# Earlier loads of the raw output weights, and two queued operations a step, in an encoder block

## The chip, the cores and the metric

The kernel runs on one core of a Trainium2 chip. The metric is the device time of one execution in microseconds. The median of three executions before the change is 499.15 us (498.17, 499.15, 500.5).

## What is computed

One encoder layer on 1024 tokens of width 1024, in float32. A combined projection is cut into head groups: group A is 2-D neighbourhood attention with 8 heads on a 16 x 64 grid, group B is windowed attention with 8 query and 2 key heads. Each group's output is gated, then projected, added to the input and normalised:

```python
h = jnp.einsum('bsd,de->bse', x, w_in[layer])
q_a, k_a, v_a, z_a, q_b, k_b, v_b, z_b = jnp.split(h, SPLIT_POINTS, axis=-1)
y_a = neighborhood_attention(q_a, k_a, v_a, rel_pos_bias[layer])
y_b = windowed_gqa_with_sink(rotary(q_b), rotary(k_b), v_b, sink_logits[layer])
mixed = jnp.concatenate([y_a * silu(z_a), y_b * silu(z_b)], axis=-1)
y = jnp.einsum('bse,ed->bsd', mixed, w_out[layer])
x = layer_norm(DEEPNORM_ALPHA * x + y, ln_gain[layer], ln_bias[layer])
```

(The reshapes into heads are left out here.)

## The kernel before

Every large float32 product is made of three matmuls in a reduced float format: each operand is split into a high part (a cast) and a low part (operand minus high part), and high x high, high x low and low x high are summed. So a weight has to be loaded raw, cast by ScalarE and subtracted by GpSimd or VectorE before TensorE (PE) can use it.

After a first stage (the value projection), the kernel walks 128 attention units of 128 queries each, first those of group B, then those of group A, with a software pipeline over steps i = 0 to 134. In step i:
- PE makes the scores of unit i (lines 532 and 533), the product of probabilities and values of unit i-6 (line 596), and after it a share of the "fill", matmuls that have nothing to do with the attention (`pump_to`).
- VectorE (DVE) adds the bias and finds the row maximum of unit i (line 539), and makes the low half of the probabilities of unit i-1 (line 566, "split-low").
- ScalarE (ACT) makes the high half of the probabilities of unit i-1 (line 565), scales the output of unit i-6 (line 601) and takes the exponential of unit i (line 554).
- SyncE (SP) issues every DMA in the listed order: biases four steps ahead, value windows (`va`), and for each unit a DMA transpose of the split probabilities (line 569), which line 596 needs five steps later.

The schedule is written out by hand (`tc.manual_schedule()`): every engine executes its instructions in the order in which the program emits them.

Beside this fixed frame there are four queues of small operations, for ScalarE, VectorE, GpSimd (POOL) and SyncE. `enq` puts an operation in its queue with the operations that it depends on; `pop(eng, n)` emits at most n of those that are ready, by priority, and an operation is ready when all that it depends on was emitted in an earlier step. ScalarE's queue is popped at the end of a step, behind the exponential; VectorE's behind the split-low; SyncE's queue gives one load at the start of a step, unless a bias or a value window was issued there, and then only if the load has waited over two steps. `need` emits an operation at once, where a matmul is about to use its result.

The fill is in this order: the last of the 21 column projections, `z3`, takes the steps 112 to 119 (6 matmuls a step). Then come three "heads" of the output projection, `out_head`: the first three of the eight row groups of `w_out`, in the order 4, 5, 6 (`EO`), for token tiles 0, half of 3, and 1. The first head takes the steps 120 to 125 with 3 matmuls a step, so each of these steps uses one new half of a row group: n = 0 in step 120, up to n = 5 in step 125. For each n:
- `wo_load(n)` loads the raw half (256 KB, tile `wor`, line 652), queued at step `WO_LD[n]`. The raw tiles take the places of `w_in`'s tiles (`WO_TAG`).
- `wo_split(n)`, queued at step 116 + n for n = 0 to 5, makes the high part `woh` on ScalarE (line 661) and the low part `wol` on GpSimd, or on VectorE where n is 2 or 5 (line 665).
- `m_queue(e)`, queued at the steps `M_AT`, splits the gated outputs of the row group e on ScalarE (line 680, two casts) and GpSimd (line 681).

n = 6, 7 and 8 are loaded in the loop too, but are split behind it. Behind the loop, `final` splits the other parts and makes the remaining output projection, the residual and the normalisation. Its matmuls begin with the heads for token tile 2 in the banks `ps_t`.

The two halves of `z3` are evacuated through ScalarE's queue (line 262) and VectorE (line 263) before PE may reuse their bank `ps_pj`; the second half of the first head (n = 1 is its first matmul) waits for the second of them.

## Time and profile before

| | value |
|---|---|
| median of three runs | 499.15 us |
| profiled execution | 498.68 us, span 496.9 us |
| PE matmul busy | 479.3 us (96%) |
| VectorE busy | 319.2 us (64%) |
| ScalarE busy | 279.6 us (56%) |
| GpSimd busy | 163.2 us (33%) |
| DMA | 74.74 MB, mean 150 GB/s |
| chain that ended last | PE 92% of the span |

The page cuts the span into 40 slices of 12.4 us. Each digit is the busy share in tenths; `PEclk` is the clock that was granted to PE, in tenths of full speed.

```profile
PE   8999999999999999999999999999998599999993
PEclk9999999999999999999999999999999579999997
DMA  8860001595285554847798989999799549204612
```

PE has one hole, in the slices 31 and 32 of the 40, that is 373 to 397 us, and the clock is low in the second of them and in the slice behind it. The end of the attention loop lies in this stretch: the steps 117 to 134 run from 371 to 411 us.

The waits between 360 and 497 us name the same lines (who waits and for what: us in total, times, longest):

```profile
PE ps_pj L698 <- ACT woh L661: 5.6, 3, 2.6
PEld ps_pj L698 <- POOL wol L665: 2.1, 2, 1.1
PE ps_pj L698 <- POOL wol L665: 1.1, 2, 0.6
PE ps_pj L698 <- DVE z L263: 0.8, 1, 0.8
```

"PE ... <- ACT woh L661" reads: a matmul of line 698 stood idle until ScalarE's cast of line 661 had ended.

### The profile page before, as it was taken

The numbers are of one execution on the slowest core, as the hardware profiler recorded it, in microseconds if no ns is written. First come the engines' busy times: TensorE is split into PE (matmuls) and PEld (weight loads), VectorE is DVE, ScalarE is ACT, GpSimd is POOL, SyncE is SP. The second block draws the span as 40 slices with busy tenths as digits, with TensorE's granted clock in tenths as the row PEclk, the third lists the DMA queues.
The fourth block names the chain that finished last, engine by engine and source line by source line (L and its number), as shares of the span: only waits on it lengthen the run. The fifth ranks groups of instructions, "written<-read, shape, count | busy, mean of one in ns | idle before, by whom it ended". The sixth has DMA issues, their size and how long they took to land.

```text
span 496.9 us, 9312 instructions
## 1 busy us (share of the span) xinstructions
PE 479.3 (96%) x3240; PEld 396.1 (80%) x3240; DVE 319.2 (64%) x788; ACT 279.6 (56%) x723; POOL 163.2 (33%) x152
## 2 busy tenths in 40 slices
PE   8999999999999999999999999999998599999993
PEld 7999988887887778878788788888886378888883
DVE  5718216778578778787777667656666239659545
ACT  5641133423788778888787878767788434012102
POOL 0030012695254174552133143123253204306423
PEclk9999999999999999999999999999999579999997
DMA  8860001595285554847798989999799549204612
GB/s 259 286 234 0 1 21 44 158 289 162 65 132 118 128 108 102 143 108 137 176 184 176 191 182 230 204 210 232 146 213 233 110 116 306 102 1 149 219 56 85
DMA packets 132383, 74.74 MB, mean 150 GB/s; under 512 B 101104, under 2 KB 117488, under 8 KB 132080
## 3 DMA queue, kind: packets, MB, share of 16 engines
q1 hardware_dynamic: 132192, 74.00, 62.7%
q8 instruction: 25, 0.41, 0.3%
q14 instruction: 22, 0.18, 0.1%
q10 hardware_dynamic: 144, 0.15, 0.1%
HBM read 43.72 MB, written 9.96 MB: 108 GB/s over the span
## 4 chain that ended last, share of the span: by engine, by line
PE 92%; DVE 3%; ACT 1%; issue 1%; POOL 1%; DMA 1%; SPq 0%; POOLq 0%; DVEq 0%; ACTq 0%
PE ps_pj L291 45%; PE ps_s L698 7%; PE ps_t L596 7%; PE ps_pj L698 5%; PE ps_t L698 4%; PE ps_s L361 4%; PE ps_s L533 4%; PE ps_s L532 4%; PE ps_t L361 3%; PE ps_pj L361 3%; PE ps_ot L698 2%; PE ps_ot L610 2%; PE ps_ot L361 1%; DVE rp_raw L238 1%; DVE ks L210 1%
## 5 line engine op out<-in xcount | busy, mean ns | idle before, releaser
L291 PE MATMUL ps_pj<-xl,wh 128*128 128x512 f32 x336 | 139.5, 415 | 0.0
L291 PE MATMUL ps_pj<-xh,wh 128*128 128x512 f32 x336 | 133.2, 396 | 0.5 <-ACT rp_raw L234 0.5
L291 PE MATMUL ps_pj<-xh,wl 128*128 128x512 f32 x336 | 132.0, 393 | 0.0
L153 POOL TENSOR_TENSOR wl<-wr,wh 128x512 fp32r<-128x512 f32 x42 | 56.3, 1342 | 172.4 <-ACT wh L149 154.3
L554 ACT ACTIVATE ps_s<-sn,nm 128x385 f32<-128x385 f32 (+3 forms) x128 | 70.2, 548 | 10.5 <-DVE nm L539 9.6
L291 PEld LDWEIGHTS ps_pj<-xh,wh 128*128 128x128 f32 x336 | 63.2, 188 | 9.7 <-ACT rp_raw L234 0.7
L291 PEld LDWEIGHTS ps_pj<-xh,wl 128*128 128x128 f32 x336 | 63.5, 189 | 9.2
L566 DVE SCALAR_TENSOR_TENSOR split<-ps_s,split 128x384 f16<-128x384 f32 (+2 forms) x128 | 65.6, 512 | 8.2 <-ACT split L565 7.4
L291 PEld LDWEIGHTS ps_pj<-xl,wh 128*128 128x128 f32 x336 | 63.4, 189 | 8.7
L601 ACT ACTIVATE on<-ps_t,ri 128x64 f32<-128x64 f32 x128 | 40.0, 312 | 50.2 <-PE ps_t L596 48.9
L539 DVE CUSTOM_DVE_ANT_0 sn<-ps_s,bias 128x288 f32<-128x288 f32 (+1 forms) x64 | 32.4, 506 | 50.1 <-PE ps_s L533 48.1
L596 PEld LDWEIGHTS <-tr 128*128 128x128 f16 (+1 forms) x1104 | 40.1, 99 | 26.5 <-issue 25.7
L565 ACT ACTIVATE split<-ps_s 128x384 f16<-128x384 f32 (+2 forms) x128 | 58.1, 454 | 1.6
L539 DVE CUSTOM_DVE_ANT_0 sn<-ps_s,bm,nsk 128x384 f32<-128x384 f32 (+1 forms) x64 | 37.2, 581 | 24.8 <-PE ps_s L533 24.1
L533 PE MATMUL ps_s<-ks,qs 128*128 128x384 f32 (+2 forms) x128 | 41.6, 325 | 0.0
L532 PE MATMUL ps_s<-ks,qs 128*128 128x384 f32 (+2 forms) x128 | 41.5, 324 | 0.0
L216 POOL CAST ks<-ks 64x512 fp32r<-64x512 f32 x40 | 27.2, 679 | 37.0 <-ACT ks L206 18.4
L149 ACT CAST wh<-wr 128x512 fp32r<-128x512 f32 x42 | 25.7, 613 | 11.0 <-PE ps_pj L291 8.5
L532 PEld LDWEIGHTS ps_s<-ks,qs 128*128 128x128 f32 x128 | 24.6, 192 | 5.9 <-issue 0.2
L596 PE MATMUL ps_t<-va,tr 96*128 96x64 f16 (+1 forms) x576 | 28.9, 197 | 0.2 <-DMA tr<-split 0.2
L533 PEld LDWEIGHTS ps_s<-ks,qs 128*128 128x128 f32 x128 | 24.6, 192 | 5.4
L596 PE MATMUL ps_t<-vb,tr 128*128 128x64 f16 x528 | 26.5, 194 | 0.0
(189 smaller groups left out, 878.0 us busy)
## 6 DMA issues: line engine op xcount, KB each, us to landing
wr<-in_wt SPq DMA_DIRECT2D x42, 256.0 KB, 3.2
bias<-in_bias SPq DMA_DIRECT2D x16, 288.0 KB, 3.4
wor<-in_wo SPq DMA_DIRECT2D x16, 256.0 KB, 4.4
xr<-in_x SPq DMA_DIRECT2D x8, 512.0 KB, 5.8
xraw<-in_xT SPq DMA_DIRECT2D x15, 256.0 KB, 3.9
out<-xr SPq DMA_DIRECT2D x14, 256.0 KB, 3.3
bias<-in_bias SPq DMA_DIRECT2D x8, 384.0 KB, 4.2
wvraw<-in_wv SPq DMA_DIRECT2D x7, 320.0 KB, 4.2
```

Source lines behind the costliest of these rows:

```text
L153: nc.gpsimd.tensor_sub(l, raws.pop(m), h.bitcast(F32))
L291: nc.tensor.matmul(ps, a[:, k % 4, :], b[half, k], start=(k == 0 and i == 0), stop=(k == KT - 1 and i == 2))
L361: nc.tensor.matmul(ps[:, :320], lh[t // 4, k][:, ts], rh[k][:, cs], start=(k == 0 and i == 0), stop=(k == KT - 1 and i == 2))
L532: nc.tensor.matmul(ps[:, :n], q, sl[0], start=True, stop=False)
L533: nc.tensor.matmul(ps[:, :n], q, sl[1], start=False, stop=True)
L539: nc.vector.tensor_tensor_reduce(sn[:, :n], ps[:, :n], bias_t, -1.0, init, op0=ALU.add, op1=ALU.min, accum_out=nm)
L554: nc.scalar.activation(pt[:, :m], sn[:, :m], AF.Exp, bias=nm, scale=-1.0, accum_out=sm[:, odd:odd + 1])
L565: nc.scalar.activation(hl[:, :m, 0, :c], src, AF.Copy, scale=PSCALE)
L566: nc.vector.scalar_tensor_tensor(hl[:, :m, 1, :c], src, PSCALE, hl[:, :m, 0, :c], op0=ALU.mult, op1=ALU.subtract)
L596: nc.tensor.matmul(ps[:, :HD], a, b_, start=(i == 0), stop=(i == len(mms) - 1))
L601: nc.scalar.activation(on[g, p, ti // 2][:, ti % 2, j, :], ps[:, :HD], AF.Copy, scale=ri[:, u[4]:u[4] + 1])
L698: nc.tensor.matmul(ps, lh[:, ts], rh[:, cs], start=(e == EO[0] and i == 0), stop=(e == EO[-1] and i == 2))
```

## The change

Two things change. The list of steps at which the raw halves of `w_out` are queued for loading ends at 123 instead of 131. And from step 112 (the first of `M_AT`) on, ScalarE and VectorE take two operations a step from their queues instead of one (`ND` and `NA` are 1).

```diff
-WO_LD = [111, 112, 114, 116, 120, 121, 129, 130, 131]
+WO_LD = [111, 112, 113, 114, 115, 118, 121, 122, 123]
...
-            pop("dve", ND)
+            pop("dve", ND if i < M_AT[0] else 2)
...
-            pop("act", NA)
+            pop("act", NA if i < M_AT[0] else 2)
```

The steps at which the splits are queued (`WO_AT`, `M_AT`) and the fill's steps stay as they are, so PE's instructions keep their order.

## The prediction

> **What bounds the kernel now.** I read the page's 40 slices first: TensorE (PE) is busy nearly everywhere except one hole at 380 to 400 us, where the granted clock also falls. I then cut that hole into stretches. Columns: stretch, its length, then busy time of PE, weight load, VectorE (DVE), ScalarE (ACT), GpSimd (POOL), the granted clock, DMA share, GB/s.

> ```profile
> 378.75:382.17 3.42, 2.58 (x28) 2.03 (x27) 2.34 (x7) 2.79 (x9) 0.07 (x1) 1.00 0.99 213
> 382.17:385.58 3.41, 1.53 (x14) 0.95 (x13) 1.92 (x7) 2.45 (x8) 2.01 (x2) 1.00 1.11 277
> 385.58:389.00 3.42, 1.99 (x4) 1.29 (x5) 0.11 (x1) 1.22 (x4) 1.74 (x2) 0.50 1.20 211
> ...
> 399.24:402.65 3.41, 3.41 (x22) 2.69 (x22) 1.45 (x7) 1.24 (x4) 0.00 (x0) 0.50 0.26 58
> 402.65:406.06 3.41, 3.41 (x39) 2.44 (x36) 1.31 (x6) 1.87 (x6) 0.00 (x0) 1.00 0.26 60
> ```

> PE was busy 1.53 of 3.41 us in the second stretch, the clock was 0.50 from 385.58, and came back at 402.65, right after a stretch in which PE was busy throughout: five stretches, 17.07 us, at half clock. One stretch with 2.58 busy kept the full clock. Next, the timeline shows what PE waited for (start, length, engine, line, operation; in brackets its idle time and who ended it):

> ```profile
> 379.18 0.58 ACT L262 ACTIVATE z<-ps_pj 128x512 f32<-128x512 f32 x1
> 380.53 0.49 PE L698 MATMUL ps_pj<-woh,ks 128*128 128x512 f32 x1 [0.83 <-DVE z L263]
> 385.80 0.61 ACT L661 CAST woh<-wor 128x512 fp32r<-128x512 f32 x1
> 386.46 0.79 PE L698 MATMUL ps_pj<-woh,ks 128*128 128x512 f32 x1 [2.57 <-ACT woh L661]
> 387.81 0.80 PE L698 MATMUL ps_pj<-wol,ks 128*128 128x512 f32 x1 [0.55 <-POOL wol L665]
> 391.68 0.80 PE L698 MATMUL ps_pj<-woh,qs 128*128 128x512 f32 x1 [1.51 <-ACT woh L661]
> 396.89 0.80 PE L698 MATMUL ps_pj<-woh,qs 128*128 128x512 f32 x1 [1.50 <-ACT woh L661]
> ```

> These are steps 121 (n=1) and 123, 124, 125 (n=3, 4, 5): weight parts made in the very step that uses them. From step 120's scores (377.68) to the first L698 matmul into `ps_t` (410.79) are 33.11 us with PE busy 25.41, so 7.7 idle. Of the busy time 12.08 us (1.99+1.90+2.43+2.35+3.41, the five slow stretches) ran at half clock. A 512-column matmul follows its neighbour by 0.43 us there and by 0.233 at full clock, a ratio of 0.545, so 5.5 us were lost to the clock. **Losses to win back: 7.7 + 5.5 = 13.2 us.** Behind 410.79 PE is busy without a gap to about 489: that part has its own order, which is unchanged, and moves as a block.

> SyncE's queue (SPq), which issues every DMA, in the steps 117 to 121:

> ```profile
> 375.18 0.58 SPq L652 DMA_DIRECT2D wor<-in_wo  x1
> ...
> 377.12 0.59 SPq L465 DMA_DIRECT2D va<-vwin  x1
> 377.75 0.48 SPq L509 DMA_DIRECT2D bias<-in_bias  x1
> 378.34 2.79 SPq L569 DMA_TRANSPOSE tr<-split  x2
> 381.18 0.57 SPq L652 DMA_DIRECT2D wor<-in_wo  x1
> ```

> The first is n=3, the last n=4. Landings, asked for issue by issue: n=3 after 3.5 us (378.7), the bias 5.0 (382.75), the first transpose 5.1 (383.4), the next 4.4 (384.3), n=4 3.6 (384.8). So landings follow each other by 0.5 to 0.9 us: the DMA is full here.

> **The change, part by part.** The order listings of both kernels have the same instructions on every engine; PE's order is identical. So nothing is added or removed, only waits move.

> *ScalarE.* Eight casts move. High parts of n=0 to 5 stand in steps 116, 117, 118, 119, 120, 121 instead of 117, 118, 119, 123, 124, 125; the two casts of mixed group 6 in 118 and 119 instead of 121 and 122. One cast holds ScalarE 0.51 us (373.26 to 373.77). In steps 112 to 118 that fits: where a step gets one more, ScalarE had 0.5 us of waiting for PE right behind (0.52 before 372.45, 0.54 before 376.65), or a later step has one fewer (113, 115). Without this cover it would cost 0.5 us a step.
> *GpSimd, VectorE.* Low parts of n=3 and 4 (1.27 us each) run in steps 120 and 121, where GpSimd stood idle 4.95 us; n=2 and 5 (0.68) run on VectorE in steps 119 and 122; all are three steps ahead of their use. Cost 0, and PE's waits of 2.57, 0.55, 1.51, 0.55 and 1.50 us (6.7 together) go.
> *SyncE.* By the listing n=0 to 3 keep their places; n=4 goes from step 120 to 118, n=5 from 121 to 119, and n=6, 7, 8 from behind the last transpose to steps 121, 123, 124. Each issue takes 0.57 us plus 0.06, ahead of transposes of 1.21 us that VectorE's split-low and the product of six steps later hang on.

> **Where a new stall goes.** ScalarE works strictly in the listed order, so a cast whose load hasn't landed stops everything behind it.
> (a) Step 119: the cast of n=3 stands at 377.9 (exponential and one cast from 376.86), but n=3 lands at 378.7. It ends at 379.35, the exponential of 120 runs at 379.86, the z cast at 380.4 instead of 379.18, VectorE's z product ends 381.7, and PE's wait before n=1 grows from 0.83 to about 2.0.
> (b) Step 120: n=4 now is issued at 378.3, behind the bias. Its landing isn't in the trace. Bounds: 3.5 us (the fastest wor nearby) gives 381.8; 5.4 (n=2's, issued at 369.70) gives 383.7. I take 383.5, since the bias ahead of it lands at 382.75. ScalarE waits from 380.9 to 383.5, splits unit 120 to 384.5, VectorE follows to 385.0, and PE's scores of unit 123, which need that PSUM bank, start near 385.1 (382.74 now).
> (c) From 385.1 on all weight parts are ready. PE still has 5 score pairs (3 of 0.36, 2 of 0.26), 11 products of 0.28, 36 matmuls of 0.233 with 0.09 more behind each product, and 4 pairs of PE transposes at 0.25: 1.6+3.1+8.4+1.0+1.0 = 15.1, to 400.2. SyncE has, from unit 120's transpose at 385.0, eight transposes (1.27 with gap), one bias and two loads (0.63): 12.1 to 397.1, and the last lands 2.5 to 3.5 later than its issue, near 399; behind it come 1.2 us of PE work. Both ends agree on 400.2. ScalarE needs about 1.5 us a step (0.51+0.09+0.48+0.21 with small waits), less than it has. I add 0.5 for waits on transposes.
> (d) Clock: the stretch 378.75 to 382.17 would have about 2.0 idle, PE busy 1.4, less than the 1.53 that lowered the clock before. So one stretch at half clock, in which the slow matmuls fill the wait of (b) and PE is busy throughout, and back at 385.58. It costs 3.41 x 0.455 = 1.55 in a stretch without cover, 0 if all lies under (b). I take 1.0, since the grid of stretches need not lie the same in another execution.

> End of the block: 400.2 + 0.5 + 1.0 = 401.7 in place of 410.79, a gain of 9.1. The profiled execution took 498.68 (span 496.9 and 1.8 around it): 489.6. The median of the runs, 499.15, lies 0.5 above it: **490.1 us**.

> [...]

> **The rivals.**
> 1. *The clock holds.* For it: 2.58 busy kept it, and my 1.4 busy is an estimate. Then the 1.0 of (d) falls away: 489.1. [...]
> 2. *The loads are in time.* If n=3 and n=4 land in 2.5 us, like the last transposes at 400 us, (a) stays at 0.83 and (b) goes: losses about 1.3 instead of 4.1, 487.3. Against it: nothing lands in under 3.5 us with the DMA at a share of 1.0 to 1.2.
> 3. *The clock stays low.* If (a), (b) and waits on transposes keep each stretch below full, as 2.43 busy did, five stretches cost 5 x 1.55 = 7.75 instead of 1.0: 496.9. For it: PE was busy 2.35 and 2.43 there and the clock stayed down. Against: at half clock PE has 2.4 us of work a step (1.33/0.545) and is the slowest engine, so it fills a stretch.
> 4. *SyncE blocks: slower.* The bias at 372.23 took 1.58 us to issue instead of 0.5, one transpose 1.99 instead of 1.21. If the five earlier loads fill the queue so that each costs SyncE 1.1 more (5.5) and each of the 11 transposes from unit 117 on 0.8 more (8.8), the last product moves 14.3 later than 400.2, to 414.5: 3.7 behind now, 502.9. It decides from 10.6 us of such blocking on. Against: one long bias issue in steps 111 to 121.
> 5. *No effect.* ScalarE might wait for loads as long as PE waits for casts now: 499. It needs n=4 to land 9 us later than in (b); the longest landing of that tensor is 6.7 in all.

> **How the numbers follow.** Chances: forecast 0.48, clock holds 0.20, in time 0.07, clock low 0.14, slower 0.06, no effect 0.05. The runs of this kernel differ by 0.47%, so 0.5% (2.5 us) is what can be told from no change. Faster takes the first three and, of the clock that stays low, the part with fewer than five stretches (0.10; 496.9 itself lies at 0.45%): 0.85. Same is the rest of that and no effect: 0.09; slower 0.06. The range begins at 487, where everything lands almost in time, and reaches to 495.5 (three low stretches more and n=4 landing an extra microsecond late); that leaves out most of rival 3, 4 and 5, about 0.2.

> **What would show it.** Right: no PE wait on L661's ScalarE cast or on L665 for n=3, 4, 5; ScalarE waiting for DMA at L661 in steps 119 and 120, 0.8 and 2 to 3 us; PE's wait before n=1 near 2; the first `ps_t` matmul of L698 near 402; at most two stretches at half clock; 78 us from there to PE's end as now. Wrong: PE waiting on transposes for more than 2 us in all, transposes on SyncE taking over 1.3 us, or a clock of 0.50 beyond 395.

## The result, and the profile after

The changed kernel takes 492.23 us (median of four runs, 489.69 to 493.54); the kernel before took 499.38 beside it. The ratio is 0.985, with a 95% interval of 0.9817 to 0.9882: faster by 1.5%. Two later series of the same kernel gave 490.85 and 490.95. The profiled execution took 491.25, its span 489.5.

The page's slices, the same three rows as before:

```profile
PE   8999999999999999999999999999999789999993
PEclk9999999999999999999999999999999899999998
DMA  7861001586285545746799899999879998104612
```

The hole of 373 to 397 us has become a dent, and the clock is low for a part of one slice only. DMA is now busy through the whole end of the loop.

Busy times of two stretches, in the columns of the prediction: from the scores of unit 120 to the first L698 matmul into `ps_t`, and from there to the end:

```profile
377.68:403.31 25.63, 21.12 (x197) 15.69 (x195) 11.44 (x36) 14.84 (x45) 3.87 (x4) 0.93 1.02 212
403.31:489.50 86.19, 78.06 (x366) 64.87 (x363) 56.92 (x103) 15.30 (x28) 30.48 (x23) 0.97 0.37 124
```

The first stretch took 33.11 us before, so it is 7.48 shorter, and the span is 7.4 shorter: the whole gain lies here. PE's idle time in it fell from 7.70 to 4.51 us and its busy time from 25.41 to 21.12, for the same 197 matmuls. So 3.2 us of the gain are waits, and 4.3 are work that no longer runs at half clock. The second stretch is as long as before (86.1 us from 410.79 to the end of the span).

Who waited in the timeline of the stretch (PE, ScalarE, VectorE; start, length, and in brackets the idle time and its end):

```profile
379.57 0.62 ACT L661 CAST woh<-wor 128x512 fp32r<-128x512 f32 x1 [1.58 <-DMA wor<-in_wo]
381.11 0.59 ACT L262 ACTIVATE z<-ps_pj 128x512 f32<-128x512 f32 x1
381.74 0.69 DVE L263 SCALAR_TENSOR_TENSOR z<-z,ps_pj 128x512 f32<-128x512 f32 x1 [0.68 <-ACT z L262]
382.48 0.57 PE L698 MATMUL ps_pj<-woh,ks 128*128 128x512 f32 x1 [2.78 <-DVE z L263]
384.26 0.62 ACT L661 CAST woh<-wor 128x512 fp32r<-128x512 f32 x1 [2.55 <-DMA wor<-in_wo]
385.22 0.46 DVE L566 SCALAR_TENSOR_TENSOR split<-ps_s,split 128x288 f16<-128x288 f32 x1 [2.42 <-ACT split L565]
391.58 0.50 PE L698 MATMUL ps_s<-woh,ks 128*128 128x512 f32 x1 [0.40 <-DVE split L566]
394.10 0.44 PE L596 MATMUL ps_t<-va,tr 96*128 96x64 f16 x9 [0.44 <-DMA tr<-split]
397.55 0.44 PE L596 MATMUL ps_t<-va,tr 128*128 128x64 f16 x9 [0.76 <-DMA tr<-split]
```

PE's waits of 2.57, 1.51 and 1.50 us on ScalarE's casts are gone. In their place ScalarE stands before the casts of n=3 (1.58) and n=4 (2.55) until their loads land. The first passes through the z cast (L262) and VectorE's product (L263) to PE, whose wait before n=1 grew from 0.83 to 2.78. Later PE waits twice for a transpose.

The clock, in the stretches of its grid:

```profile
379.34:382.75 3.41, 0.63 (x11) 0.51 (x11) 1.54 (x5) 2.13 (x6) 1.30 (x2) 1.00 1.06 268
382.75:386.17 3.42, 3.42 (x17) 2.66 (x17) 0.98 (x5) 1.91 (x6) 1.22 (x1) 0.50 1.14 233
386.17:389.58 3.41, 3.41 (x36) 2.60 (x36) 2.53 (x8) 3.21 (x11) 0.06 (x1) 1.00 0.98 226
```

PE was busy 0.63 of 3.41 us in the first, ran at half clock in the second, was busy throughout there, and had the full clock again in the third: one slow stretch in place of five.

### The profile page after: what moved, and what is told of

It is laid out like the page before. It is cut to its first block, busy times and chain, and to the rows that moved or that the text cites. A ratio compares the mean times of both kernels' runs of the same rounds, so it can differ in the third digit from the quotient of the medians.

```text
span 489.5 us, 9314 instructions
## 1 busy us (share of the span) xinstructions
PE 474.4 (97%) x3240; PEld 392.6 (80%) x3240; DVE 320.2 (65%) x788; ACT 280.1 (57%) x723; POOL 163.4 (33%) x152
## 4 chain that ended last, share of the span: by engine, by line
PE 89%; DVE 4%; DMA 3%; ACT 2%; issue 1%; SPq 1%; DVEq 0%; ACTq 0%
PE ps_pj L291 45%; PE ps_t L596 6%; PE ps_s L698 6%; PE ps_t L698 4%; PE ps_s L361 4%; PE ps_pj L698 4%; PE ps_s L533 4%; PE ps_s L532 4%; PE ps_t L361 3%; PE ps_pj L361 3%; PE ps_ot L698 2%; PE ps_ot L610 2%; PE ps_ot L361 1%; DMA tr<-split 1%; DMA wor<-in_wo 1%
```

## The experiments

"Stretch" is from the scores of unit 120 to the first matmul into `ps_t`, in the profiled execution of each kernel; "idle" is the stretch minus PE's busy time; "slow" counts half-clock stretches of 3.41 us in it. The ratios are to the kernel before in the same series. A blank line separates series on different occasions.

| kernel | stretch us | idle us | slow | median us | ratio, 95% interval |
|---|---|---|---|---|---|
| before | 33.11 | 7.70 | 5 | 499.38 | 1 |
| changed | 25.63 | 4.51 | 1 | 492.23 | 0.985 (0.9817 to 0.9882) |
| | | | | | |
| changed, again | 24.97 | 4.00 | 1 | 490.85 | 0.9859 (0.9835 to 0.9882) |
| two operations a step, old loads | 24.04 | 2.83 | 1 | 490.17 | 0.9852 (0.983 to 0.9874) |
| new loads, one operation a step | 31.48 | 7.08 | 4 | 497.84 | 0.9997 (0.9978 to 1.0016) |
| late casts | 23.51 | 3.91 | 0 | 490.41 | 0.9859 (0.9829 to 0.989) |
| | | | | | |
| late casts, late tail | 22.12 | 2.60 | 0 | 488.55 | 0.9779 (0.9751 to 0.9806) |
| late tail | 24.42 | 3.18 | 1 | 490.53 | 0.9823 (0.9799 to 0.9846) |
| early loads | 23.56 | 2.71 | 1 | 489.86 | 0.9811 (0.9785 to 0.9837) |
| ScalarE only | 25.27 | 3.01 | 2 | 491.38 | 0.9838 (0.9814 to 0.9862) |
| | | | | | |
| early loads, late casts, late tail | 22.83 | 2.91 | 0 | 488.67 | 0.9794 (0.977 to 0.9818) |
| old loads, late casts | 24.19 | 3.20 | 1 | 490.28 | 0.9814 (0.9791 to 0.9838) |
| late casts, late tail, again | 21.26 | 1.80 | 0 | 489.32 | 0.98 (0.9774 to 0.9825) |
| changed, again | 24.82 | 4.66 | 0 | 490.95 | 0.984 (0.9815 to 0.9865) |

The start of the stretch itself moves between 377.6 and 380.1 us from profile to profile, with the code in front of it almost the same. Hence the stretch tells kernels apart better than the total time does. It comes from one profile of each row, though: the three profiles of the changed kernel lie 0.8 us apart (24.82 to 25.63), the two of the late casts with late tail 0.9, so a difference of that size between two rows isn't evidence.

### Which half of the change wins

Two operations a step, old load steps (against the changed kernel):

```diff
-WO_LD = [111, 112, 113, 114, 115, 118, 121, 122, 123]
+WO_LD = [111, 112, 114, 116, 120, 121, 129, 130, 131]
```

> Two queued operations a step as in the changed kernel, loads at the old steps. Theory (the gain is that the casts leave PE's path; the earlier loads only set how long ScalarE stands before a cast): nearly the whole gain stays, 489.5 to 493.5 us; ScalarE stands at the casts of n=3 and n=4 for a load (about 1.5 and 2 us), no PE wait on a cast of n=3, 4, 5. Rival (the gain is the earlier loads, which let the final part find its raw halves sooner): 498 to 500.

The other half alone (against the kernel before):

```diff
-WO_LD = [111, 112, 114, 116, 120, 121, 129, 130, 131]
+WO_LD = [111, 112, 113, 114, 115, 118, 121, 122, 123]
```

> Loads at the new steps, one queued operation a step as before. Theory: no gain, 498 to 501 us, the PE waits of 2.57, 1.51 and 1.50 us on ScalarE's casts stay and so do about five slow stretches of the clock; up to 1 us lost because five loads stand ahead of transposes. Rival (earlier loads): 490 to 493.

Both came out as the theory said, but for sizes: the loads alone, at 497.84 us, lie just under their range, in a series where the kernel before took 498.09. The two operations a step alone give a ratio of 0.9852, the whole change gives 0.9859 in the same series; the loads alone give 0.9997, no difference. The timeline of the first shows ScalarE's casts of n=3, 4 and 5, each waiting for its load, and none of PE waiting for them:

```profile
380.65 0.62 ACT L661 CAST woh<-wor 128x512 fp32r<-128x512 f32 x1 [0.84 <-DMA wor<-in_wo]
386.31 0.62 ACT L661 CAST woh<-wor 128x512 fp32r<-128x512 f32 x1 [1.76 <-DMA wor<-in_wo]
388.75 0.62 ACT L661 CAST woh<-wor 128x512 fp32r<-128x512 f32 x1 [0.71 <-DMA wor<-in_wo]
```

In the second (the loads alone) PE waits for the casts as before, in the same three steps:

```profile
385.70 0.50 PE L698 MATMUL ps_pj<-woh,ks 128*128 128x512 f32 x1 [1.76 <-ACT woh L661]
390.92 0.80 PE L698 MATMUL ps_pj<-woh,qs 128*128 128x512 f32 x1 [1.50 <-ACT woh L661]
396.14 0.80 PE L698 MATMUL ps_pj<-woh,qs 128*128 128x512 f32 x1 [1.50 <-ACT woh L661]
```

So a raw half that is loaded earlier is worth nothing while its cast stands where it stood.

ScalarE alone, VectorE at one operation (against the changed kernel):

```diff
-            pop("dve", ND if i < M_AT[0] else 2)
+            pop("dve", ND)
```

> The changed kernel with VectorE back at one queued operation a step. Theory: VectorE's queue has only the low parts of n=2 and 5 here, so nothing changes beyond the spread: 490 to 492 us. Rival (both engines' second operation counts): 493 or more.

491.38 us, a ratio of 0.9838: as the changed kernel. VectorE's second operation a step does nothing that can be measured. (Besides the low parts of n=2 and 5, the two products of `z3` pass through its queue in these steps.) This kernel and the one with the loads alone differ only in ScalarE's second queued operation, and their ratios, each to the kernel before in its own series, are 0.9838 and 0.9997: so of the three edits, that one makes the gain. The other two were each left out alone and not missed; a kernel without both wasn't run.

### Taking ScalarE's waits for loads away

Late casts (against the changed kernel): the splits of n=3, 4, 5 are queued at 120, 122, 123. By the listed order their casts then stand in these steps instead of 119, 120, 121.

```diff
-WO_AT = 116
+WO_AT = [116, 117, 118, 120, 122, 123]
...
-            if WO_AT <= i < WO_AT + 6:
-                wo_split(i - WO_AT)
+            if i in WO_AT:
+                wo_split(WO_AT.index(i))
```

> As the changed kernel, but the splits of n=3, 4, 5 are queued at the steps 120, 122, 123 instead of 119, 120, 121, so that their loads have landed when ScalarE comes to the cast. Theory: ScalarE's waits of 1.6 and 2.6 us for loads go, PE's wait before n=1 falls from 2.8 back to about 0.8, the clock has no slow stretch; 1.5 to 4 us faster than the changed kernel on the same chip, 487.5 to 490.5. Rival (SyncE's transposes set the end of the loop whatever ScalarE does): the same as the changed kernel within 1 us, with PE's waits on transposes grown by what the other waits lost.

The waits went as expected. No cast of ScalarE waits for a load any more, PE's wait before n=1 falls to 1.07 us, and this profile has no slow stretch. But the median, 490.41 against 490.85, is lower by less than the runs of one kernel differ, and the stretch is shorter by only 1.5 us. Other waits have come (VectorE and PE in this kernel's timeline):

```profile
382.75 0.56 DVE L539 CUSTOM_DVE_ANT_0 sn<-ps_s,bias 128x384 f32<-128x384 f32 x1 [1.24 <-DMA bias<-in_bias]
390.27 0.46 DVE L539 CUSTOM_DVE_ANT_0 sn<-ps_s,bias 128x288 f32<-128x288 f32 x1 [1.43 <-DMA bias<-in_bias]
...
384.16 0.43 PE L596 MATMUL ps_t<-va,tr 128*128 128x64 f16 x9 [0.62 <-DMA tr<-split]
391.39 0.40 PE L532 MATMUL ps_s<-ks,qs 128*128 128x288 f32 x1 [1.23 <-DVE split L566]
395.48 0.44 PE L596 MATMUL ps_t<-va,tr 128*128 128x64 f16 x9 [0.82 <-DMA tr<-split]
```

VectorE now waits for the biases of the units 122 and 126, and PE for two transposes. The second bias is issued behind the load of n=6, with one transpose between them, and lands 4.5 us after its issue. PE's 1.23 us at 391.39 is VectorE's 1.43, passed on through split-low. The rival had a part of the truth here: waits for the DMA take over.

Late tail, with the late casts and without them: n=6, 7, 8 are loaded behind the last transpose again.

```diff
-WO_LD = [111, 112, 113, 114, 115, 118, 121, 122, 123]
+WO_LD = [111, 112, 113, 114, 115, 118, 129, 130, 131]
```

> The late casts of n=3, 4, 5 (steps 120, 122, 123) and the loads of n=6, 7, 8 back at the steps 129 to 131, behind the last transpose. In the profile of the late casts VectorE stood 1.43 us for the bias of unit 126, issued right behind the load of n=6, and PE 0.8 us for a transpose. Theory (the three loads in the loop take DMA time from bias and transposes and give nothing): both waits shrink below 0.5 us, the stretch from the scores of unit 120 to the first matmul into ps_t takes 21.5 to 23 us instead of 23.5, median 0.5 to 2 us below the late casts. Rival (the final part needs n=6, 7, 8 early): a PE wait on weight parts behind the loop, 1 us or more slower.

> The changed kernel with only the loads of n=6, 7, 8 back at the steps 129 to 131. Theory: ScalarE's waits for n=3 and n=4 (1 to 1.6 and 1.9 to 2.6 us) stay, PE's waits on transposes (0.9 and 0.7) go: 24 to 25 us for the stretch instead of 25.0 to 25.6, 489.5 to 491 us. Rival (these loads are what wins): 493 or more.

With the late casts: 488.55 us and a stretch of 22.12, in the expected range; the wait for the bias of unit 126 is gone: issued at 387.18, it is taken up by VectorE at 391.28, 4.1 us later, without a wait. Not as expected, VectorE still waits for the bias of unit 122 (1.90 us) and PE for one transpose (1.15). Behind the loop PE waits for nothing, so the final part doesn't need n=6, 7, 8 early. Without the late casts: 24.42 and 490.53, as expected; ScalarE's waits stay (0.88 and 3.06 us), and one of PE's waits on transposes remains, 0.36 us.

Early loads: the casts of the changed kernel, but raw halves issued sooner (by the listed order n=0, 1, 3, 4 leave SyncE in the steps 108, 111, 115, 117).

```diff
-WO_LD = [111, 112, 113, 114, 115, 118, 121, 122, 123]
+WO_LD = [107, 109, 112, 113, 114, 118, 129, 130, 131]
```

> Casts as in the changed kernel, but n=0, 1, 3, 4 loaded earlier: SyncE issues n=0 in step 108, n=1 in 111, n=3 in 115 instead of 117, n=4 in 117 instead of 118, n=6, 7, 8 behind the loop. Theory: ScalarE's wait for n=3 goes and that for n=4 falls below 1 us, PE's wait before n=1 falls to about 0.8 to 1.1, no slow stretch of the clock; stretch 21.5 to 23.5 us, 487.5 to 490. Rival (the crowded DMA delays a transpose as much as the load gains): as the changed kernel, 490 to 492.

Half right. No cast of n=3 or n=4 waits for its load any more, and PE's wait before n=1 is 1.10. But now the cast of n=5 stops ScalarE: its load, issued at 380.24, lands after 4.6 us.

```profile
384.82 0.62 ACT L661 CAST woh<-wor 128x512 fp32r<-128x512 f32 x1 [3.10 <-DMA wor<-in_wo]
```

So the stall moved to the next load, which the edit had not moved forward. Against the expectation the clock falls once. Total and stretch lie between the changed kernel and the late casts with late tail.

Both remedies together, and old loads with late casts (the late casts' `WO_AT` in each):

```diff
-WO_LD = [111, 112, 113, 114, 115, 118, 121, 122, 123]
+WO_LD = [107, 109, 112, 113, 114, 120, 129, 130, 131]
```

> Both remedies together: casts of n=3, 4, 5 in the steps 120, 122, 123, loads of n=0, 1, 3, 4 earlier (steps 108, 111, 115, 117), n=5 in 120, n=6 to 8 behind the loop. Theory (what is left in the late casts with late tail is 1.2 us of PE waiting for a transpose that stands behind the loads of n=4 and 5 in the full DMA): that wait falls below 0.6, stretch 21 to 22.2 us, 0 to 1 us below the late casts with late tail. Rival (any load moved ahead of the bias of units 122 to 125 makes that bias late): VectorE waits 1.5 us or more for the bias, stretch 22.5 or more.

```diff
-WO_LD = [111, 112, 113, 114, 115, 118, 121, 122, 123]
+WO_LD = [111, 112, 114, 116, 120, 121, 129, 130, 131]
```

> All loads at the steps of the kernel before, two operations a step, casts of n=3, 4, 5 in the steps 120, 122, 123. Theory (the earlier loads are worth nothing by themselves): 22 to 23.5 us for the stretch, ScalarE waiting 0 to 1.5 us for n=4; within 1 us of the late casts with late tail, 488 to 490. Rival (n=4 and 5 must be loaded earlier): ScalarE waits 2 us or more, a slow stretch of the clock, 490.5 or more.

The first gave the waits and the stretch that its rival named: no cast waits for a load, but VectorE waits 2.67 us for the bias of unit 122, PE 1.31 for a transpose, and the stretch is 22.83. That the earlier loads made this bias late isn't shown: VectorE waited for it in both profiles of the late casts with late tail too, 1.90 and 1.28 us. The second is undecided. ScalarE waits only 0.61 us for a load, as the theory had it, but VectorE waits 3.45 for the bias of unit 122, PE 2.06 for a transpose, the clock falls once, and the stretch of 24.19 is outside the range that was given. Up to that bias SyncE's order is the one of the kernel before and of the kernel with two operations a step and old loads. From the issue of the bias to the end of VectorE's wait for it went 6.2 us here (379.42 to 385.62) and 5.15 in the kernel before (377.75 to 382.90); with two operations a step and old loads VectorE used it 5.2 us after its issue (379.71 to 384.91) and its wait there was for PE. So this transfer came about 1 us later in one profile than in another at the same place in SyncE's order, and one profile doesn't rank these variants.

The late casts with late tail and the changed kernel, side by side:

> The late casts with late tail again, beside the changed kernel on the same chip: 1.5 to 3 us below it, 487.5 to 489.5, no slow stretch of the clock within the loop.

> The changed kernel again: 490 to 492.5 us, one or two slow stretches of the clock.

489.32 against 490.95 us, stretches of 21.26 and 24.82. Against its expectation the changed kernel had no slow stretch this time. The ratios, 0.98 (0.9774 to 0.9825) and 0.984 (0.9815 to 0.9865), overlap a little. The late casts with late tail have the shortest stretch in both series and no slow stretch in either profile, and their median is 1.6 us below the changed kernel's here. The kernel with both remedies, at 488.67 (0.977 to 0.9818), can't be told from them. So these two are the best kernels here, but their lead on the changed kernel is about the size of what the intervals resolve.

## Why the prediction was right, point by point

The forecast was 490.1 us, the range 487.0 to 495.5, and 492.23 was measured. The mechanism was right; two terms were too small, and one was counted twice.

- *Where the time is won: right.* All PE waits on L661's and L665's products for n=3, 4, 5 are gone (waits of 0.2 to 0.4 us on a low part appear in some variants only), the part behind the first `ps_t` matmul kept its length (86.1 and 86.2 us), and the loads alone changed nothing.
- *(a), too small.* PE's wait before n=1 was forecast at about 2.0 and was 2.78. The chain is the one that was named: n=3's cast waits, then the z cast, the z product and PE. n=3 was issued at 375.73 instead of 375.18 and landed in 3.8 us instead of 3.5. In the two later profiles of the same kernel PE waited 2.37 and 1.91, so the forecast lies within what the three profiles show, and this one at the upper end. The sum starts behind (b) and holds (a) in no term of its own.
- *(b), right.* Forecast: n=4 lands at 383.5, 5.2 us after its issue, ScalarE waits 2.6, VectorE is done with unit 120 at 385.0. Measured: 5.4 us to landing, a wait of 2.55, done at 385.7. It is 0.7 later because n=4 was issued at 378.83 instead of 378.3 and took 0.2 longer.
- *(d), right in this profile.* One slow stretch was forecast, because PE would be busy only 1.4 us between 378.75 and 382.17; it was 0.63 between 379.34 and 382.75, and the slow stretch followed. The grid lay 0.6 us later. PE reached the scores of unit 123 at 386.24, 0.55 behind VectorE's 385.7: that is what the slow clock cost where it mattered, against the 1.0 that I took.
- *(c), too small.* From there to 403.31 went 17.07 us; the work was put at 15.1 and the waits at 0.5. The waits were 0.40 (split-low), 0.44 and 0.76 (transposes), 1.6 together; the other 15.5 are work, 0.4 more than the forecast. The DMA's share over the stretch was 1.02, where it had been 0.65. I had counted SyncE's issue times and left the crowding of the DMA in a term of half a microsecond. That the crowding made these two transposes late is argued, not shown by a run: with the late tail one of these waits remains, 0.36.
- *The sum:* 386.24 instead of 385.1 is +1.14, 17.07 instead of 15.6 is +1.47, and the separate 1.0 for the clock, already in the first, goes: +1.6, which is 403.31 instead of 401.7. It was luck that this 1.0 hid a part of the two shortfalls, which are 2.6 together. The rest of the distance to 492.23 is that this median lies 1.0 above the profiled execution, where I took 0.5; the medians of the two later series lie within 0.9 of the forecast.
- *The rivals.* The clock holds: not in the profile of the result, but in the last one of the same kernel, whose stretch was 24.82 against 24.97 and 25.63 with a slow stretch; so as far as three profiles show, its price is 1 us or less, as forecast. Loads in time: no, they took 3.8 and 5.4 us. Clock low throughout, no effect: neither happened. SyncE blocking: not in the sum, but SyncE was held at single issues. A value window took 2.12 us instead of 0.57, and three transposes took 1.66, 1.89 and 1.93 instead of 1.21. So one of the signs given for being wrong, transposes of over 1.3 us, did appear; the three held SyncE 1.8 us longer together, far from the 10.6 at which that rival decides.

One thing I hadn't asked: whether the first edit matters at all. I costed the earlier loads as delays for transposes and as a condition of the gain. The runs show that they are no condition of it: n=4 and 5 issued two steps later serve as well, since a cast is ready only when its load was issued in an earlier step, and these two casts then stand one step later too (121 and 122).

## What to carry to other kernels

When an engine waits for a small operation of a helper engine, look at that engine's queue policy first: here eight casts of 0.51 us stood one to a step, and a second one per step was the whole gain, while loading their inputs earlier alone gave 0.9997. Where an engine executes in the listed order, as ScalarE does here, a cast that it meets before the load has landed passes the wait on to what stands behind it (ScalarE's 1.58 us before the cast of n=3 came with 2.78 us of PE's before n=1 instead of 0.83). So place casts by the landing under the DMA load of that stretch (3.5 to 5.4 us here for raw halves, with the DMA at a share of 1.0 to 1.3), not by the issue. Whether a load that is moved forward makes another transfer late wasn't shown: the bias of unit 126, one transpose behind the load of n=6, landed after 4.5 us in the late casts and after 3.5 in the changed kernel. But n=6, 7 and 8 behind the last transpose cost nothing (stretches of 22.12 us against 23.51, and 24.42 against 24.82 to 25.63), so loads that nobody needs yet can stand behind the transfers that others wait for.

## What the runs showed of the hardware

When PE's clock falls can be read, within limits, off the 14 profiles, in the stretches of 3.413 us in which the clock changes (half clock lasted one of them in the profile after, 382.75 to 386.17, and five, 17.07 us, in the one before, 385.58 to 402.65). In the end of the loop at full clock, stretches with PE busy 0.63, 1.08, 1.09, 1.33, 1.36, 1.38, 1.54, 1.56 and 1.85 us were each followed by half clock; those with 2.17 us or more never. Two with 1.68 and 1.86 kept the full clock, so in between it isn't settled. These two lines are from different kernels, the early loads (fell behind it) and the changed kernel's last profile (didn't fall):

```profile
383.51:386.93 3.42, 1.85 (x20) 1.21 (x21) 1.71 (x6) 2.07 (x6) 0.00 (x0) 1.00 1.12 257
```

```profile
380.41:383.82 3.41, 1.68 (x15) 1.39 (x16) 1.37 (x5) 1.04 (x4) 0.78 (x1) 1.00 1.15 251
383.82:387.23 3.41, 2.71 (x20) 1.57 (x20) 1.93 (x6) 3.38 (x11) 1.27 (x1) 1.00 1.14 297
```
